# Ring slots 64 bytes longer, transposed rows 64 bytes apart: a four-layer transformer trunk on one Trainium2 core

## The chip, the cores and the metric

The kernel runs on one core of one Trainium2 chip, as one launch. The metric is the device time of one execution in microseconds (us). Engines are named as in the profile: PE is TensorE (matrix products), PEld its weight loads, DVE is VectorE, ACT is ScalarE, POOL is GpSimd, SP issues most of the DMAs.

## The reference, cut to what matters

A decoder trunk of four layers over 256 positions and a model width of 1024, all in float32. Layer i uses one token mixer (i mod 3: differential attention, stick-breaking attention, windowed attention with sinks), and then a SwiGLU feed-forward block of hidden width 2816. Each sub-layer sits between two RMS norms:

```python
for i in range(DEPTH):                                   # 4
    hn = rms_norm(x, norm_gains[i, 0])
    m = mixer[i % 3](hn, ...)                            # h @ w_in, attention, @ w_out
    x = x + rms_norm(m, norm_gains[i, 1])
    f = swiglu(rms_norm(x, norm_gains[i, 2]), w_gate[i], w_up[i], w_down[i])
    x = x + rms_norm(f, norm_gains[i, 3])

def swiglu(h, w_gate, w_up, w_down):
    return (jax.nn.silu(h @ w_gate) * (h @ w_up)) @ w_down
```

Nearly all of the arithmetic is in the products with the weights, and these are read once from memory: some 200 MB in float32.

## The kernel before, in words

The 256 positions are two **streams** of 128 rows, s = 0 and s = 1. Both run through all layers; stream 1 follows stream 0 by at most LAG = 8 weight units, so that each weight is loaded and prepared once and used by both.

**Weights.** The weights are cut into 378 units of 128 partitions by 1024 float32 (4096 bytes a partition). `load_dma` brings unit u into one of four `stage` tiles. `split` makes two tiles out of it in a ring of RING = 11 slots each: ACT copies the unit into `hi`, of type float32r, which rounds it, and DVE subtracts, so that `lo = stage - hi` holds what the rounding took away.

**Activations.** `pre_norm` transposes a stream's rows on PE and splits them in the same way into `xh` (high part) and `xl` (low part), 128 partitions by 8 blocks of 128. The feed-forward block's hidden rows become `hTh` and `hTl`, the attention outputs `oh` and `ol`.

**Products.** A product with weights is three float32r matmuls: high rows by `hi`, high rows by `lo`, low rows by `hi`. The weights are the moving operand (512 columns as a rule, 256 in the projections of layer 2), the transposed rows are the stationary one, a block of 128 by 128 loaded by a weight load of its own ahead of each matmul. `project` does the projections and gate/up, six matmuls a unit and stream: for each of two blocks `xh` by `hi` and `xh` by `lo`, then twice `xl` by `hi`. `rows_product` does the output projection and the down projection, six matmuls a unit and stream too. From the code there are 72 units of the first kind in layers 0, 1 and 3, 44 x 4 gate/up units, 8 x 4 output units and 22 x 4 down units, each used by both streams: 864 + 2112 + 384 + 1056 = 4416 matmuls of 512 columns; layer 2 adds 10 units of 24 matmuls over both streams with 256 columns, 240.

**Where the tiles lie.** Pools lay their tiles out one after another along each partition. Ring slots, stage tiles, `xh` and `xl` take 4096 bytes, the temporaries of the tag `t2k` 2048 (TMP = 8 buffers, which rotate in the order of allocation), `junk` 2048, the `o` tiles 2048. So before the change all operands of these matmuls start a multiple of 512 bytes apart. `junk` takes the elementwise output of sums of squares, which nobody reads; it has one buffer, and ACT alone writes it.

**Order.** `Emitter` emits both streams in the order of a simple model of PE's time: a stream that needs a weight unit goes on when the unit is in the ring, and tasks (transposes, scores, values of the attention) are spawned with a delay. `act`, `dve`, `pool` and `pe` are wrapped in `Start`: while its switch is on (until stream 1's first norm) instructions keep program order, after that the framework's scheduler may move them; its model decides the order within each engine's queue. On the chip each queue runs strictly in that order.

In the profile nearly every instruction has one line, that of the wrapper (L181), so groups are told apart by tiles: `mm_f` is gate/up, `acc_f` the down projection, `mm_a`, `mm_b`, `mm_c` projections of the mixers, `acc_a` and so on their output projections, `tp` transposes of x, `th_f` transposes of the hidden rows.

Of the kernel before, what the change touches and what calls it, by code (L numbers as in the profile page):

```python
# [10 lines left out]
F32R = mybir.dt.float32r  # L11
BF16 = mybir.dt.bfloat16
# [6 lines left out]
P = 128  # L19
D = 1024  # L20
KT = D // P
# [6 lines left out]
THETA = 10000.0  # L28

RING = 11  # L30
STAGE = 4
AHEAD = 3
LAG = 8
TMP = 8
# [6 lines left out]
class Emitter:  # L41
# [27 lines left out]
    def advance(self):  # L69
        free = self.pos[1] + RING  # L70
        while self.loaded < min((self.pos[0] + AHEAD if self.pos[0] else 2), free, self.limit):
            self.fetch(self.loaded + STAGE)
            self.ring[self.loaded] = self.split(self.loaded)
            self.loaded += 1
# [83 lines left out]
def trunk_kernel(ctx, tc, x, positions, norm_gains, a_w_in, a_w_out, a_lambda, a_subln, b_w_in, b_w_out,  # L158
                 c_w_in, c_w_out, c_sinks, w_gate, w_up, w_down, out, depth=DEPTH):
    nc = tc.nc  # L160
    cst = ctx.enter_context(tc.tile_pool(name="cst", bufs=1))
    ringp = ctx.enter_context(tc.tile_pool(name="ringp", bufs=RING))
    stagep = ctx.enter_context(tc.tile_pool(name="stagep", bufs=STAGE))
    wk = ctx.enter_context(tc.tile_pool(name="wk", bufs=2))
    sm = ctx.enter_context(tc.tile_pool(name="sm", bufs=2))
# [2 lines left out]
    def bank(tag, s, shape, name):  # L168
        return ps.tile(shape, F32, tag=f"{tag}{s}", name=name, bufs=BANKS[tag])
# [82 lines left out]

    def split(u):
        t = staged.pop(u)
        hi = ringp.tile([P, 1024], F32R, tag="hi", name=f"hi_{u}")
        lo = ringp.tile([P, 1024], F32R, tag="lo", name=f"lo_{u}")
        act.activation(hi, t, AF.Copy)
        dve.tensor_tensor(lo, t, hi.bitcast(F32), ALU.subtract)
        return hi, lo

    em = Emitter(load_dma, split, len(units), edges)


# [109 lines left out]
    def mm(o, a, b, start, stop, f32=False):  # L373
        pe.matmul(o, a, b, start=start, stop=stop)
        n = 1
        for d in o.shape[1:]:
            n *= d
        em.t += n * COLUMN_NS * (4 if f32 else 1)
# [6 lines left out]
    def transpose(o, i):  # L385
        pe.transpose(o, i, ident)
        em.t += P * COLUMN_NS * 4

    def rstd_of(name, s, ss, more=EPS, extra=None):

        u = sm.tile([P, 1], F32, tag=f"u{s}", name=f"u_{name}")
        r = sm.tile([P, 1], F32, tag=f"r{s}", name=f"r_{name}", bufs=3)
        pool.tensor_scalar(u, ss, more, extra, ALU.add, *([ALU.add] if extra else []))
        pool.tensor_tensor(r, u, mhalf[:, 0:1], ALU.pow)
        return r

    def first_halves(s, tps, gs, th, tl, name):

        ys = []
        for half in range(2):  # L400
            y = wk.tile([P, 4, P], F32, tag="t2k", name=f"y_{name}_{half}", bufs=TMP)
            dve.tensor_tensor(y, tps[half], gs[half].unsqueeze(2).to_broadcast([P, 4, P]), ALU.mult)
            ys.append(y)
            if s == 0:
                next(rope_tables)
        for half in range(2):
            hs = slice(4 * half, 4 * half + 4)
            act.activation(th[:, hs, :], ys[half], AF.Copy)
            dve.tensor_tensor(tl[:, hs, :], ys[half], th[:, hs, :].bitcast(F32), ALU.subtract)
            if s == 0:  # L410
                for _ in rope_tables if half else range(2):
                    next(rope_tables, None)
                em.limit = half + 1
                em.advance()
        em.limit = len(units)

    def pre_norm(s, n, name):

        ss = sm.tile([P, 1], F32, tag=f"ss{s}", name=f"ss_{name}")
        th = wk.tile([P, KT, P], F32R, tag=f"xh{s}", name=f"xh_{name}", bufs=1)  # L420
        tl = wk.tile([P, KT, P], F32R, tag=f"xl{s}", name=f"xl_{name}", bufs=1)
        tps, gs = [], []
        for half in range(2):
            tp = bank(("tp", "mm")[half], s, [P, 4, P], f"tp_{name}_{half}")
            for j in range(4):
                kt = 4 * half + j
                transpose(tp[:, j, :], xs[s][:, kt * P:(kt + 1) * P])
            tps.append(tp)
            gs.append(gains[:, n * KT + 4 * half:n * KT + 4 * half + 4])
        if act.on:  # L430
            first_halves(s, tps, gs, th, tl, name)
        else:
            for half in range(2):
                for j in range(4):
                    act.activation(th[:, 4 * half + j, :], tps[half][:, j, :], AF.Copy, scale=gs[half][:, j:j + 1])
                for j in range(4):
                    kt = 4 * half + j
                    dve.scalar_tensor_tensor(tl[:, kt, :], tps[half][:, j, :], gs[half][:, j:j + 1], th[:, kt, :].bitcast(F32),
                                             ALU.mult, ALU.subtract)
        junk = wk.tile([P, D], BF16, tag="junk", name=f"junk_{name}", bufs=1)  # L440
        act.activation(junk, xs[s], AF.Square, scale=1.0 / 32, accum_out=ss)
        return th, tl, rstd_of(name, s, ss)

# [11 lines left out]

    def post_norm(s, acc, gain, name):
        ss = sm.tile([P, 2], F32, tag=f"ssp{s}", name=f"ssp_{name}")
        junk = wk.tile([P, D], BF16, tag="junk", name=f"junk_{name}", bufs=1)
        mg = [wk.tile([P, 512], F32, tag="t2k", name=f"mg_{name}{h}", bufs=TMP) for h in range(2)]
        for h in range(2):  # L460
            act.activation(junk[:, h * 512:(h + 1) * 512], acc[h], AF.Square, scale=1.0 / 32, accum_out=ss[:, h:h + 1])
        r = rstd_of(name, s, ss[:, 0:1], ss[:, 1:2], EPS)
        for h in range(2):
            dve.tensor_tensor(mg[h], acc[h], gain[:, h * 512:(h + 1) * 512], ALU.mult)
        for h in range(2):
            cs = slice(h * 512, (h + 1) * 512)
            dve.scalar_tensor_tensor(xs[s][:, cs], mg[h], r, xs[s][:, cs], ALU.mult, ALU.add)
# [95 lines left out]
    def split_rows(oT, sl, src, scale=None):  # L563

        hi, lo = oT[0][:, sl, :], oT[1][:, sl, :]
        if scale is None:
            act.activation(hi, src, AF.Copy)
            dve.tensor_tensor(lo, src, hi.bitcast(F32), ALU.subtract)
        else:
            act.activation(hi, src, AF.Copy, scale=scale)  # L570
            dve.scalar_tensor_tensor(lo, src, scale, hi.bitcast(F32), ALU.mult, ALU.subtract)

    def layer_a(s, i, xn):
        inst = i // 3
        name = f"a{i}{s}"
# [64 lines left out]
        def values(g):  # L640
            yield ("e", (name, "w", g))
            if s:
                yield ("e", (f"a{i}0", "v", g))
            yield ("d", 500)
            o = bank("tp", s, [P, 4, P], f"pv_{name}{g}")
            for h in range(4):
                for kb in range(nk):
                    mm(o[:, h, :], wT[g][:, h, kb, :], V[g, kb][:, h * P:(h + 1) * P], kb == 0, kb == nk - 1, True)
            ss = sm.tile([P, 4], F32, tag=f"os{s}", name=f"os_{name}{g}")
            junk = wk.tile([P, D], BF16, tag="junk", name=f"junk_{name}{g}", bufs=1)  # L650
            for h in range(4):
                act.activation(junk[:, h * P:(h + 1) * P], o[:, h, :], AF.Square, accum_out=ss[:, h:h + 1])
            dve.scalar_tensor_tensor(ss, ss, 1.0 / P, st[g, "el"], ALU.mult, ALU.add)
            pool.tensor_tensor(ss, ss, mhalf[:, 0:4], ALU.pow)
            on = wk.tile([P, 4, P], F32, tag="t2k", name=f"on_{name}{g}", bufs=TMP)
            dve.tensor_tensor(on, o, ss.unsqueeze(2).to_broadcast([P, 4, P]), ALU.mult)
            yield ("d", 4200)
            tp = bank("tp", s, [P, 4, P], f"to_{name}{g}")
            for h in range(4):
                transpose(tp[:, h, :], on[:, h, :])  # L660
            split_rows(oT[g], slice(0, 4), tp, gsub[:, inst:inst + 1])
            yield ("d", 900)
            for h in range(4):
                em.set((name, "o", 4 * g + h))
# [288 lines left out]
```

## Time and profile before

| | us |
|---|---|
| median of 2 runs (1204.61 to 1205.26) | 1204.93 |
| the profiled execution | 1205.73 |
| its span, first to last instruction | 1203.9 |
| PE busy | 1185.8 (98%) |
| PE weight loads busy | 971.6 (81%) |
| DVE busy | 779.2 (65%) |
| ACT busy | 656.9 (55%) |

The granted clock of TensorE was 0.998 over the span. A busy share of PE counts from a matmul's start to its modelled end, so matmuls overlap in it; how fast PE goes is read from one start to the next. Idle time of DVE and ACT costs nothing as long as PE does not wait for them. The profiled execution's time is 1.8 us above its span.

### The profile page before, as it was taken

What the parts mean: (1) busy time and instruction counts of PE and PEld (TensorE: products, weight loads), DVE (VectorE), ACT (ScalarE), POOL (GpSimd) and SP (SyncE); (2) the same over time, 40 slices, a digit from 0 to 9 for tenths busy, and PEclk for the clock granted to TensorE, in tenths of its full rate; (3) what the DMA queues carried; (4) which work ended last, traced back from release to release, by engine and by line L of the source; (5) the groups of instructions that cost most, each with busy time, mean ns of one, the idle gap of its engine ahead of it and who ended that gap; (6) DMA issues with size and microseconds to landing.
All of it is one profiled execution on the core that took longest, in us unless ns stands there. A gap on an engine that the chain in (4) does not pass through costs nothing.

```text
span 1203.9 us, 16738 instructions
## 1 busy us (share of the span) xinstructions
PE 1185.8 (98%) x6028; PEld 971.6 (81%) x6028; DVE 779.2 (65%) x1217; ACT 656.9 (55%) x1197; POOL 48.1 (4%) x141
## 2 busy tenths in 40 slices
PE   8999999999999999999999999999999999999997
PEld 7787888888878888888888778888888788888886
DVE  7876765555847666555588666655587776655553
ACT  5665644444756665444476655444475565544442
POOL 2000100000200000000000000000010001000000
PEclk9999999999999999999999999999999999999999
DMA  8635465565644546656664246555565453566550
GB/s 280 206 120 159 151 192 186 189 192 179 225 139 123 176 140 193 191 181 189 192 199 135 88 144 191 191 189 187 185 205 156 129 175 123 179 189 192 180 170 35
DMA packets 140838, 205.90 MB, mean 171 GB/s; under 512 B 9554, under 2 KB 104916, under 8 KB 140756
## 3 DMA queue, kind: packets, MB, share of 16 engines
q1 hardware_dynamic: 140048, 204.51, 54.0%
q8 instruction: 47, 0.77, 0.3%
q10 hardware_dynamic: 708, 0.34, 0.1%
q14 instruction: 35, 0.29, 0.1%
HBM read 203.76 MB, written 1.05 MB: 170 GB/s over the span
## 4 chain that ended last, share of the span: by engine, by line
PE 90%; DVE 3%; ACT 3%; issue 2%; POOL 1%; DMA 1%; ACTq 0%; DVEq 0%; POOLq 0%
PE mm_f L181 39%; PE acc_f L181 18%; PE acc_a L181 3%; PE mm_c L181 2%; PE acc_b L181 2%; PE sc_a L181 2%; PE th_f L181 2%; DVE lo L181 1%; PE acc_c L181 1%; PE sc_b L181 1%; DMA stage<-in_a_w_in_dram 1%; ACT hi L181 1%; PE pv_a L181 1%; PE sc_c L181 1%; PE pv_c L181 1%
## 5 line engine op out<-in xcount | busy, mean ns | idle before, releaser
L181 DVE TENSOR_TENSOR lo<-stage,hi 128x1024 fp32r<-128x1024 f32 x378 | 461.0, 1223 | 285.5 <-ACT hi L181 283.6
L181 ACT ACTIVATE hi<-stage 128x1024 fp32r<-128x1024 f32 x378 | 399.5, 1061 | 324.1 <-PE mm_f L181 154.4
L181 PE MATMUL mm_f<-hi,xh_q 128*128 128x512 f32 x704 | 280.2, 398 | 0.0
L181 PE MATMUL mm_f<-lo,xh_q 128*128 128x512 f32 x704 | 274.5, 390 | 0.0
L181 PE MATMUL mm_f<-hi,xl_q 128*128 128x512 f32 x704 | 217.4, 390 | 1.0 <-DVE xl_q L181 1.0
L181 PEld LDWEIGHTS mm_f<-hi,xl_q 128*128 128x128 f32 x704 | 132.2, 188 | 30.4 <-DVE xl_q L181 1.9
L181 PEld LDWEIGHTS mm_f<-hi,xh_q 128*128 128x128 f32 x704 | 132.2, 188 | 26.1 <-ACT xh_q L181 0.2
L181 PEld LDWEIGHTS mm_f<-lo,xh_q 128*128 128x128 f32 x704 | 132.4, 188 | 25.8
L181 PE MATMUL acc_f<-hi,hTh_f 128*128 128x512 f32 x352 | 113.7, 399 | 0.5 <-ACT hTh_f L181 0.5
L181 PE MATMUL acc_f<-hi,hTl_f 128*128 128x512 f32 x352 | 111.4, 392 | 0.5 <-DVE hTl_f L181 0.4
L181 PE MATMUL acc_f<-lo,hTh_f 128*128 128x512 f32 x352 | 110.7, 390 | 0.0
L181 ACT ACTIVATE t_f<-mm_f,half_f 128x256 f32<-128x256 f32 x88 | 41.7, 474 | 79.7 <-PE mm_f L181 79.7
L181 PEld LDWEIGHTS acc_f<-hi,hTl_f 128*128 128x128 f32 x352 | 65.9, 188 | 14.9 <-DVE hTl_f L181 1.0
L181 PEld LDWEIGHTS acc_f<-lo,hTh_f 128*128 128x128 f32 x352 | 66.1, 188 | 14.0
L181 PEld LDWEIGHTS acc_f<-hi,hTh_f 128*128 128x128 f32 x352 | 63.7, 188 | 11.9 <-ACT hTh_f L181 0.8
L181 DVE SCALAR_TENSOR_TENSOR t_f<-t_f,mm_f 128x256 f32<-128x256 f32 x88 | 36.7, 417 | 35.2 <-ACT t_f L181 35.1
L181 DVE SCALAR_TENSOR_TENSOR h_f<-t_f,hsq_f,mm_f 128x256 f32<-128x256 f32 x88 | 42.3, 480 | 2.7
L181 ACT ACTIVATE hTh_f<-th_f 128x256 fp32r<-128x256 f32 x88 | 33.0, 375 | 17.0 <-PE th_f L181 16.7
L181 DVE TENSOR_TENSOR hTl_f<-th_f,hTh_f 128x256 fp32r<-128x256 f32 x88 | 36.5, 418 | 5.6 <-ACT hTh_f L181 5.3
L181 ACT ACTIVATE e_a<-sc_a,nm_a 128x128 f32<-128x128 f32 (+1 forms) x64 | 26.0, 420 | 17.1 <-DVE nm_a L181 16.9
L181 PE MATMUL th_f<-ident,h_f 128*128 128x128 f32 x176 | 33.5, 271 | 0.0
L181 PEld LDWEIGHTS th_f<-ident,h_f 128*128 128x128 f32 x176 | 24.1, 139 | 11.4 <-DVE h_f L181 0.3
(584 smaller groups left out, 1543.1 us busy)
## 6 DMA issues: line engine op xcount, KB each, us to landing
stage<-in_ffn_w_gate_dram SPq DMA_DIRECT2D x176, 256.0 KB, 2.9
stage<-in_ffn_w_up_dram SPq DMA_DIRECT2D x176, 256.0 KB, 3.1
stage<-in_ffn_w_down_dram SPq DMA_DIRECT2D x88, 512.0 KB, 3.5
stage<-in_a_w_in_dram SPq DMA_DIRECT2D x48, 512.0 KB, 3.8
stage<-in_b_w_in_dram SPq DMA_DIRECT2D x24, 512.0 KB, 3.6
stage<-in_a_w_out_dram SPq DMA_DIRECT2D x16, 512.0 KB, 3.9
stage<-in_c_w_in_dram SPq DMA_DIRECT2D x10, 512.0 KB, 3.6
gain<-in_norm_gains_dram SPq DMA_DIRECT2D x8, 512.0 KB, 4.1
```

Source lines behind the costliest of these rows:

```text
L181: i = call(*args, **kw)
```

## The change: what it does

Three edits.

- **The ring.** Each of the 22 tiles of the ring gets a tag of its own, with one buffer, instead of 11 rotating buffers of the tags `hi` and `lo`. A tile has 1040 elements, of which 1024 are used, so each takes 4160 bytes, and `hi` and `lo` of a slot now lie beside each other. The last slot's `hi` has 80 elements more (320 bytes). The ring is as deep as before. Counted in steps of 64 bytes modulo 512, ring tiles now start at all eight places.
- **The rows.** `xl` of stream 0 takes 4160 bytes, so that all that lies behind it, with stream 1's `xh` and `xl`, is shifted by 64 bytes more. Counted in the same steps, stream 0's `xh` and `xl` start at place 5 and stream 1's at place 6; before, all started at place 2, as did every ring tile.
- **The space.** `junk` loses its own 2048 bytes and takes a buffer of the rotating tag `t2k` at each use.

```diff
+SLOT = 1040
...
-    ringp = ctx.enter_context(tc.tile_pool(name="ringp", bufs=RING))
+    ringp = ctx.enter_context(tc.tile_pool(name="ringp", bufs=1))
...
     def split(u):
         t = staged.pop(u)
-        hi = ringp.tile([P, 1024], F32R, tag="hi", name=f"hi_{u}")
-        lo = ringp.tile([P, 1024], F32R, tag="lo", name=f"lo_{u}")
+        hi, lo = (ringp.tile([P, SLOT + pad], F32R, tag=f"{n}{u % RING}", name=f"{n}_{u}")[:, :1024]
+                  for n, pad in (("hi", 80 * (u % RING == RING - 1)), ("lo", 0)))
         act.activation(hi, t, AF.Copy)
         dve.tensor_tensor(lo, t, hi.bitcast(F32), ALU.subtract)
         return hi, lo
...
         th = wk.tile([P, KT, P], F32R, tag=f"xh{s}", name=f"xh_{name}", bufs=1)
-        tl = wk.tile([P, KT, P], F32R, tag=f"xl{s}", name=f"xl_{name}", bufs=1)
+        tl = wk.tile([P, SLOT if s == 0 else D], F32R, tag=f"xl{s}", name=f"xl_{name}", bufs=1)
+        tl = tl[:, :D].rearrange("p (k n) -> p k n", n=P)
...
-        junk = wk.tile([P, D], BF16, tag="junk", name=f"junk_{name}", bufs=1)
+        junk = wk.tile([P, D], BF16, tag="t2k", name=f"junk_{name}", bufs=TMP)
```

The last pair of lines stands at three places: `pre_norm`, `post_norm` and the values of layers 0 and 3.

The number and kinds of instructions on every engine stay the same. The scheduler's order changes at a few places, most of them in the first 60 us; POOL and SP keep theirs. The first is in ACT's queue, where the first four weight units have been copied and stream 1's first norm begins. The names are those of the text above with the unit's number (`hi_5` is unit 5; `xh_n01` is stream 1's first `xh`, in two halves; the last number only counts tiles). Before:

```order
L181 ACTIVATE hi_2_286<-stage_2_236 128x1024
L181 ACTIVATE hi_3_292<-stage_3_238 128x1024
L181 ACTIVATE xh_n01_297<-y_n01_0_309 128x512
L181 ACTIVATE xh_n01_297<-y_n01_1_311 128x512
L181 ACTIVATE junk_n01_317,ss_n01_296<-x_1_111 128x1024
L181 ACTIVATE hi_4_331<-stage_4_251 128x1024
L181 ACTIVATE hi_5_368<-stage_5_284 128x1024
L181 ACTIVATE hi_6_380<-stage_6_290 128x1024
```

And now, in the same place of ACT's queue:

```order
L182 ACTIVATE hi_2_286<-stage_2_236 128x1024
L182 ACTIVATE hi_3_292<-stage_3_238 128x1024
L182 ACTIVATE hi_5_368<-stage_5_284 128x1024
L182 ACTIVATE xh_n01_297<-y_n01_0_309 128x512
L182 ACTIVATE xh_n01_297<-y_n01_1_311 128x512
L182 ACTIVATE junk_n01_317,ss_n01_296<-x_1_111 128x1024
L182 ACTIVATE hi_4_331<-stage_4_251 128x1024
L182 ACTIVATE hi_6_380<-stage_6_290 128x1024
```

The copy of unit 5 now stands ahead of stream 1's rows, and ahead of unit 4. DVE's queue follows at the same place of the program; before:

```order
L181 TENSOR_TENSOR y_n01_0_309<-tp_n01_0_299,gains_191 128x512
L181 TENSOR_TENSOR y_n01_1_311<-tp_n01_1_304,gains_191 128x512
L181 TENSOR_TENSOR xl_n01_298<-y_n01_0_309,xh_n01_297 128x512
L181 TENSOR_TENSOR xl_n01_298<-y_n01_1_311,xh_n01_297 128x512
L181 TENSOR_TENSOR t1_a000q_384<-mm_a000q_277,crq_a00_269 128x512
```

And now, where `t1_a000q` (the first rotated queries of stream 0) comes later:

```order
L182 TENSOR_TENSOR y_n01_0_309<-tp_n01_0_299,gains_191 128x512
L182 TENSOR_TENSOR y_n01_1_311<-tp_n01_1_304,gains_191 128x512
L182 TENSOR_TENSOR lo_5_369<-stage_5_284,hi_5_368 128x1024
L182 TENSOR_TENSOR xl_n01_298<-y_n01_0_309,xh_n01_297 128x512
L182 TENSOR_TENSOR xl_n01_298<-y_n01_1_311,xh_n01_297 128x512
```

Here `lo` of unit 5 has moved ahead of both halves of stream 1's `xl`.

More of the change, by code (lines that the diff above doesn't have):

```diff
@@ L457, in post_norm @@
         ss = sm.tile([P, 2], F32, tag=f"ssp{s}", name=f"ssp_{name}")
-        junk = wk.tile([P, D], BF16, tag="junk", name=f"junk_{name}", bufs=1)
+        junk = wk.tile([P, D], BF16, tag="t2k", name=f"junk_{name}", bufs=TMP)
         mg = [wk.tile([P, 512], F32, tag="t2k", name=f"mg_{name}{h}", bufs=TMP) for h in range(2)]
@@ L649, in values @@
             ss = sm.tile([P, 4], F32, tag=f"os{s}", name=f"os_{name}{g}")
-            junk = wk.tile([P, D], BF16, tag="junk", name=f"junk_{name}{g}", bufs=1)
+            junk = wk.tile([P, D], BF16, tag="t2k", name=f"junk_{name}{g}", bufs=TMP)
             for h in range(4):
```

## The prediction

> **What bounds the kernel now.** I read the page first: busy times, the clock by slices, the chain that ended last.
>
> ```profile
> span 1203.9 us, 16738 instructions
> PE 1185.8 (98%) x6028; PEld 971.6 (81%) x6028; DVE 779.2 (65%) x1217; ACT 656.9 (55%) x1197; POOL 48.1 (4%) x141
> PEclk9999999999999999999999999999999999999999
> PE 90%; DVE 3%; ACT 3%; issue 2%; POOL 1%; DMA 1%; ACTq 0%; DVEq 0%; POOLq 0%
> L181 DVE TENSOR_TENSOR lo<-stage,hi 128x1024 fp32r<-128x1024 f32 x378 | 461.0, 1223 | 285.5 <-ACT hi L181 283.6
> L181 ACT ACTIVATE hi<-stage 128x1024 fp32r<-128x1024 f32 x378 | 399.5, 1061 | 324.1 <-PE mm_f L181 154.4
> L181 PE MATMUL mm_f<-hi,xh_q 128*128 128x512 f32 x704 | 280.2, 398 | 0.0
> L181 PE MATMUL mm_f<-hi,xl_q 128*128 128x512 f32 x704 | 217.4, 390 | 1.0 <-DVE xl_q L181 1.0
> ```
>
> PE is busy 98% of the span and 90% of the chain. DVE and ACT are idle 35% and 45% of the time; DVE's `lo` waits for ACT's `hi`, and half of the wait of `hi` is for PE, which frees ring slots: the ring is full, and weights are not what PE waits for. In the two groups of gate/up matmuls shown the idle time of PE is 0.0 and 1.0 us over 704 instructions each. So the time is PE's pace, and a change pays only through that pace, or through PE's few stalls.
>
> The pace is read from starts, in the timeline of PE, in the middle of a feed-forward block and just behind it (columns: start, length, what, count):
>
> ```profile
> 300.56 0.39 PE L181 MATMUL mm_f<-hi,xh_q 128*128 128x512 f32 x1
> 301.02 0.39 PE L181 MATMUL mm_f<-hi,xh_q 128*128 128x512 f32 x1
> 301.47 0.62 PE L181 MATMUL mm_f<-hi,xl_q 128*128 128x512 f32 x2
> 302.83 0.62 PE L181 MATMUL acc_f<-hi,hTl_f 128*128 128x512 f32 x2
> 303.88 0.48 PE L181 MATMUL mm_f<-hi,xh_q 128*128 128x512 f32 x1
> 304.20 0.39 PE L181 MATMUL mm_f<-lo,xh_q 128*128 128x512 f32 x1
> 305.36 0.61 PE L181 MATMUL acc_f<-hi,hTh_f 128*128 128x512 f32 x2
> ```
>
> From 300.56 to 302.83 ten matmuls of 512 columns start (four by `xh`, two by `xl`, four by `hTh`): 2.27 us, 227 ns each (226.9 in a longer stretch below). The 4416 such matmuls make 4416 x 0.2269 = 1002 us, 83% of the span. After small transposes have come between, from 304.20 to 305.36, five starts take 1.16 us, 232 ns each, before the old pace is back. Layer 2 has matmuls of 256 columns, and the first microseconds ran slower:
>
> ```profile
> 670.64 0.28 PE L181 MATMUL mm_c<-hi,xh_n 128*128 128x256 f32 x1
> 671.36 0.64 PE L181 MATMUL mm_c<-hi,xl_n 128*128 128x256 f32 x4
> 11.43 0.63 PE L181 MATMUL mm_a000q<-hi,xh_n 128*128 128x512 f32 x1
> 12.29 1.05 PE L181 MATMUL mm_a000q<-hi,xl_n 128*128 128x512 f32 x2
> 1189.69 0.62 PE L181 MATMUL acc_f<-hi,hTh_f 128*128 128x512 f32 x2
> 1193.32 0.62 PE L181 MATMUL acc_f<-hi,hTl_f 128*128 128x512 f32 x2
> ```
>
> At 670 us six starts take 0.72 us, 120 ns each for 256 columns; near the end sixteen starts take 3.63 us, 226.9 ns each. So 256 more columns cost 226.9 - 120 = 106.9 ns, and each matmul carries 120 - 106.9 = 13.1 ns that its columns don't explain. At 11.43 us two starts take 0.86 us, 430 ns each, where the columns alone, 213.8 ns at the later pace, would take 428 at half of it: at that slow pace hardly anything of the 13.1 ns shows. Those 13.1 ns are the stake of this change. While a matmul streams its weights out of SBUF, the load of the next stationary block reads there too; if these two reads get in each other's way, addresses can matter. Stake: (4416 + 240) x 13.1 ns = 61 us.
>
> **The change, part by part.** *Places of operands.* Before, every float32r operand starts a multiple of 512 bytes from every other one. Within that, the ten matmuls quoted mix all that there is: `hi` and `lo`, first and second half of a slot (2048 bytes apart), two streams, rows of three tiles, and the pace doesn't move. Whole multiples of 512 bytes do nothing, then. Steps of 64 bytes below 512 don't occur before, so the trace can't show their price directly, and I bound it by rows from both sides. Below: all 13.1 ns gone, -61 us. Above: each matmul at the disturbed pace of 232 ns, 4416 x (232 - 226.9) ns = +23 us. I take 0, for two reasons. A matmul of 512 columns reads 2048 bytes while the weight load beside it reads 512, so the moving read runs through every place modulo 512 four times, wherever either starts: a shift of the start changes when they meet, not how often. And the undisturbed pace comes back by itself after an upset, and the same one in both stretches quoted: a state that the two reads settle into by timing would take in a fixed shift as well.
>
> The Trainium skill, "SBUF — State Buffer", section Specifications, gives lines of 16 bytes as the unit in which engines read, with a penalty for each access that crosses to a new line; steps of 64 bytes keep every operand at the start of such a line, so by that rule the sum gets 0 from this edit. The same page of the Trainium skill, section Who interferes with whom, has it that "PE and ACT never wait on anyone", which leaves the 13.1 ns of the rows above without a cause; the trace neither bears the rule out nor breaks it.
>
> *ACT and DVE on the new places.* `hi` takes 1061 ns and `lo` 1223 ns; both engines have a third of the span and more to spare. 5% on either would be 20 or 23 us of work beside PE: nothing on the path.
>
> *`junk` in the rotating buffers.* Nothing is added but waits: a square now waits for whoever last used a buffer handed out eight allocations ago. Each square is itself behind the product or the update that it squares, later than those old readers; 0, and at most some tenths of a microsecond at a norm, where PE goes on with the other stream. Per-tile tags of the ring keep its depth; ACT gains waits for its own long-finished copies: 0.
>
> *The order at the start.* Here there is a price. ACT's queue has `hi_5` ahead of stream 1's `xh`, and DVE's queue `lo_5` ahead of its `xl`. When does unit 5 land? The queue of SP, the window of that issue, and the engines around it:
>
> ```profile
> 13.12 0.38 SPq L246 DMA_DIRECT2D stage<-in_a_w_in_dram  x1
> stage<-in_a_w_in_dram SPq DMA_DIRECT2D x1, 512.0 KB, 6.2
> 14.11 1.06 ACT L181 ACTIVATE hi<-stage 128x1024 fp32r<-128x1024 f32 x1 [0.27 <-DMA stage<-in_a_w_in_dram]
> 17.54 1.23 ACT L181 ACTIVATE xh_n<-y_n 128x512 fp32r<-128x512 f32 x2 [2.37 <-DVE y_n L181]
> 18.20 1.30 DVE L181 TENSOR_TENSOR xl_n<-y_n,xh_n 128x512 fp32r<-128x512 f32 x2
> 19.39 0.39 PE L181 MATMUL mm_a010q<-hi,xh_n 128*128 128x512 f32 x1
> 21.61 1.22 DVE L181 TENSOR_TENSOR lo<-stage,hi 128x1024 fp32r<-128x1024 f32 x1
> ```
>
> The sixth issue, at 13.12, landed 6.2 us later, at 19.3. ACT then waits from 15.2 to 19.3, copies unit 5 until 20.4, and has the first half of `xh` (half of 1.23 us) at about 21.0; PE wants it at 19.39: 1.6 us of stall. `lo_5` then holds DVE from 20.4 to 21.6, the first half of `xl` is there at about 22.3, wanted four matmuls after 21.0, at 21.9: 0.4 us more. What is queued behind on ACT, `hi_4`, moves behind the square, to some 23 us, and `lo_4` from 21.61 to some 24; PE needs them a dozen matmuls (2.7 us) after 21.4, so they hardly bind, and the stage buffer that `lo_4` frees delays unit 8, which is wanted ten microseconds later. Loss: 2.0 us. What could take it back are PE's own stalls a little later:
>
> ```profile
> 38.19 0.72 PE L181 MATMUL sc_a<-kT_a,qT_a 64*128 64x128 f32 x8 [0.78 <-ACT kT_a L181]
> PE mm_a001k L181 <- DVE t_a001q L181: 0.7, 1, 0.7
> ```
>
> They sum to 1.5 us and hang on data that would be as late as PE itself in part; I give back 0.5. So the start costs 1.5 us, with bounds of -0.5 (both stalls closed by the new order and no loss) and 3 (the transfers bind too).
>
> **Sum.** Span 1203.9 + 0 + 1.5 = 1205.4. The profiled execution took 1205.73, 1.8 above its span and 0.8 above the median of 1204.93. On the median: 1204.9 + 1.5 = 1206.4 us.
>
> **The rivals.** *Faster: the 13.1 ns are a collision of equal places.* Then they go where places differ. For it: each matmul has them, with 512 and with 256 columns alike, they don't grow with the columns, and they are not there at the slow pace, as a collision of two reads would be hidden when one has time to spare; and before, all operands share one place out of eight. Against it: the argument of the four rounds, and that half of the stationary loads beside a matmul could be at the start and the other anywhere, yet the pace is one number. Gone altogether: 1206 - 61 = 1145. Gone for half of the pairs: 1206 - 30 = 1176. Only a fifth gone: 1194. "TensorE: Matmul & The Clock Gate" of the Trainium skill, section Wait — 56ns, gives 215.7 ns from start to start at 512 columns. The rows here show 226.9, against it; if different places brought PE to that page's pace, the change would be worth 4416 x 11.2 ns = 49 us, an estimate from that page: 1157.
>
> *Slower: the settled state is lost.* The rows at 304.20 show that there is a worse pace than 226.9, and that it takes undisturbed matmuls to get back. Now each switch from `hi` to `lo` (64 bytes), between slots and between streams shifts the places of the two reads against each other. If that keeps upsetting them, PE stays at 232 ns: 4416 x 5.1 ns = 23 us, 1229. It decides from 5.2 ns a matmul on (23 us and the start's 1.5 make 2%). Partly upset, 1 to 4 ns: 1211 to 1224. Against it: before, the operands change too at every matmul, and nothing is upset by that.
>
> *The change does nothing to PE and the start comes out even*: 1204.5, within the forecast's own range of 1204 to 1209.
>
> **How the numbers follow.** Pace unchanged, with the loss at the start: 0.60, 1204 to 1209, likeliest 1206. Faster by collisions gone: 0.24, spread from 1145 to 1204, two thirds of it beyond 2% (under 1181, about what a measurement of this kernel surely tells from no change), since a collision that depends on the place should go for more than half of the pairs. Slower by the lost state: 0.16, from 1210 to about 1236 (the 232 ns are a mean over five starts, and may be 1 or 2 ns short of the worst), some 0.07 beyond 2% (1229). So faster 0.16, same 0.77, slower 0.07. The range from 1178 to 1232 leaves out some 0.15 below and 0.05 above.
>
> **What would show it.** In the timeline of PE around 300 us: starts 226.9 ns apart, with `hi` and `lo`, both streams and all slots alike, show the first step right; 214 to 224 or a mixture that goes by slot shows the faster rival, 230 and more in stretches without transposes the slower. `hi` at 1061 ns and `lo` at 1223 ns should stand. At the start PE should wait for ACT's `xh_n` near 20 us by one to two microseconds, and ACT's `hi` ahead of it for its DMA. The prediction is wrong if the time leaves 1204 to 1209 with an unchanged pace: then the waits of `junk`, or the order, cost what I put at nothing.

## The result, and the profile after

| | before | after |
|---|---|---|
| median of 2 runs each, us | 1204.93 | 1224.05 (1223.28 to 1224.81) |
| the profiled execution, us | 1205.73 | 1224.81 |
| its span, us | 1203.9 | 1223.0 |

The changed kernel takes 1.0159 times as long, 95% interval 1.0138 to 1.0179: 19.1 us slower. The time lies in the range forecast (1178 to 1232), but outside the likeliest case's own range of 1204 to 1209.

The page of the changed kernel, the rows that answer to those of before:

```profile
span 1223.0 us, 16751 instructions
PE 1201.7 (98%) x6028; PEld 971.7 (79%) x6028; DVE 779.1 (64%) x1217; ACT 657.5 (54%) x1197; POOL 45.1 (4%) x141
PEclk8999999999999999999999999999999999999999
PE 88%; DVE 5%; ACT 2%; DMA 2%; issue 1%; POOL 1%; DVEq 0%; POOLq 0%; ACTq 0%
L182 DVE TENSOR_TENSOR lo<-stage,hi 128x1024 fp32r<-128x1024 f32 x378 | 461.0, 1223 | 299.0 <-ACT hi L182 297.9
L182 ACT ACTIVATE hi<-stage 128x1024 fp32r<-128x1024 f32 x378 | 399.5, 1061 | 339.0 <-PE mm_f L182 159.7
L182 PE MATMUL mm_f<-hi,xh_q 128*128 128x512 f32 x704 | 282.6, 401 | 0.0
```

DVE's `lo` and ACT's `hi` take what they took, 1223 and 1061 ns, and the weight loads are as long in sum (971.7 us). Busy PE alone has grown, from 1185.8 to 1201.7 us, with the same number of matmuls, and the group of `mm_f` by `hi` and `xh_q` still has no idle time. So the time went into the matmuls themselves. The timeline of PE around 300 us (columns: start, length, what, count):

```profile
301.11 0.39 PE L182 MATMUL mm_f<-hi,xh_q 128*128 128x512 f32 x1
301.34 0.40 PE L182 MATMUL mm_f<-lo,xh_q 128*128 128x512 f32 x1
301.57 0.40 PE L182 MATMUL mm_f<-hi,xh_q 128*128 128x512 f32 x1
301.81 0.39 PE L182 MATMUL mm_f<-lo,xh_q 128*128 128x512 f32 x1
302.04 0.63 PE L182 MATMUL mm_f<-hi,xl_q 128*128 128x512 f32 x2
302.51 0.63 PE L182 MATMUL acc_f<-hi,hTh_f 128*128 128x512 f32 x2
302.97 0.62 PE L182 MATMUL acc_f<-lo,hTh_f 128*128 128x512 f32 x2
303.44 0.63 PE L182 MATMUL acc_f<-hi,hTl_f 128*128 128x512 f32 x2
303.90 0.39 PE L182 MATMUL mm_f<-hi,xh_q 128*128 128x512 f32 x1
```

Twelve matmuls start between 301.11 and 303.90: 2.79 us, 232.5 ns each, where before it was 226.9. No small transposes stand between them; it is the undisturbed pace that is worse. Over the whole trace, from the starts of neighbouring 512-column matmuls (those less than 300 ns apart, some 4000 pairs), the mean is 231.73 ns against 228.03 before: 3.70 ns more, and 4416 x 3.70 ns = 16.3 us. Before, most stretches repeat steps of 227, 227 and 226 ns; after, nearly all steps lie between 224 and 241 ns, and they settle nowhere. The mean covers the pairs without a transpose between them, so 16.3 us is an estimate: the 4005 pairs alone make 14.8. This kind of mean over the starts is what "mean pace" says below.

The rest is at the start. ACT and PE of the changed kernel, from their timelines, and the busy times by windows (columns: window, its length, busy time and count of PE, PEld, DVE, ACT, POOL, then the granted clock, DMA share, GB/s):

```profile
19.67 1.06 ACT L182 ACTIVATE hi<-stage 128x1024 fp32r<-128x1024 f32 x1 [4.20 <-DMA stage<-in_a_w_in_dram]
20.63 1.14 ACT L182 ACTIVATE xh_n<-y_n 128x512 fp32r<-128x512 f32 x2
21.30 0.51 PE L182 MATMUL mm_a010q<-hi,xh_n 128*128 128x512 f32 x1 [2.00 <-ACT xh_n L182]
21.30:22.60 1.30, 1.30 (x4) 0.67 (x4) 1.30 (x3) 1.30 (x2) 0.00 (x0) 0.82 0.04 14
22.60:25.90 3.30, 3.30 (x9) 2.62 (x9) 2.53 (x7) 3.30 (x6) 1.65 (x3) 0.55 0.50 166
128.88 0.40 PE L182 MATMUL mm_f<-hi,xh_q 128*128 128x512 f32 x1
```

The same window and the same matmul (the first of layer 0's feed-forward block) before:

```profile
22.60:25.90 3.30, 3.30 (x16) 2.75 (x15) 3.30 (x9) 2.49 (x4) 1.63 (x1) 1.00 0.54 158
125.38 0.39 PE L181 MATMUL mm_f<-hi,xh_q 128*128 128x512 f32 x1
```

ACT waits 4.20 us for unit 5, PE waits 2.00 us for the rows behind it, and then, from 22.6 to 25.9, PE has 9 matmuls at work where it had 16 (one or two of them begun before 22.6), at a granted clock of 0.55 against 1.00. By 125 us the changed kernel is 3.5 us behind; the other 15.6 us of the span's 19.1 come behind that.

### The profile page after: what moved, and what is told of

It is laid out like the page before. It is cut to its first block, busy times and chain, and to the rows that moved or that the text cites. A ratio compares the mean times of both kernels' runs of the same rounds, so it can differ in the third digit from the quotient of the medians.

```text
span 1223.0 us, 16751 instructions
## 1 busy us (share of the span) xinstructions
PE 1201.7 (98%) x6028; PEld 971.7 (79%) x6028; DVE 779.1 (64%) x1217; ACT 657.5 (54%) x1197; POOL 45.1 (4%) x141
## 4 chain that ended last, share of the span: by engine, by line
PE 88%; DVE 5%; ACT 2%; DMA 2%; issue 1%; POOL 1%; DVEq 0%; POOLq 0%; ACTq 0%
PE mm_f L182 39%; PE acc_f L182 18%; PE acc_a L182 3%; DVE lo L182 2%; PE acc_b L182 2%; PE sc_a L182 2%; PE th_f L182 2%; PE acc_c L182 1%; PE mm_c L182 1%; DMA stage<-in_a_w_in_dram 1%; PE sc_b L182 1%; ACT hi L182 1%; PE pv_a L182 1%; PE sc_c L182 1%; DVE x L182 1%
## 5 line engine op out<-in xcount | busy, mean ns | idle before, releaser
L182 DVE TENSOR_TENSOR lo<-stage,hi 128x1024 fp32r<-128x1024 f32 x378 | 461.0, 1223 | 299.0 <-ACT hi L182 297.9
L182 ACT ACTIVATE hi<-stage 128x1024 fp32r<-128x1024 f32 x378 | 399.5, 1061 | 339.0 <-PE mm_f L182 159.7
L182 PE MATMUL mm_f<-hi,xl_q 128*128 128x512 f32 x704 | 220.8, 395 | 0.8 <-DVE xl_q L182 0.8
L182 PEld LDWEIGHTS acc_f<-lo,hTh_f 128*128 128x128 f32 x352 | 66.1, 188 | 15.6
L182 ACT ACTIVATE hTh_f<-th_f 128x256 fp32r<-128x256 f32 x88 | 33.1, 376 | 18.4 <-PE th_f L182 18.1
L182 ACT ACTIVATE e_a<-sc_a,nm_a 128x128 f32<-128x128 f32 (+1 forms) x64 | 26.1, 421 | 18.4 <-DVE nm_a L182 18.1
```

Of the source, the lines that this page charges most:

```text
L182: i = call(*args, **kw)
```

## The experiments

Two theories stood at first. **S**, "a lost state": PE settles into 226.7 ns only where the place of the rows against the weights never changes; any fixed shift would do, and the change keeps shifting. **D**, "distance": each distance between the start of the stationary operand (rows) and that of the moving one (weights) has a pace of its own, and 0 is a good one. A third, **W**, blames the waits and the order, not the places.

### 1. The change without its 64 bytes

```diff
-SLOT = 1040
+SLOT = 1024
...
-                  for n, pad in (("hi", 80 * (u % RING == RING - 1)), ("lo", 0)))
+                  for n, pad in (("hi", 0), ("lo", 0)))
```

> The changed kernel with slots of 4096 bytes, no longer last slot and no longer xl: per-slot tags, junk in the rotating buffers and the new order stay, but all operands start a multiple of 512 bytes apart again. If the places alone make the 19 us: about 1206 (226.9 ns a matmul again, with the 1.5 us of the start). If junk's waits, the tags or the order cost it: about 1224.

Measured: 1208.89 us, ratio 1.0029 (1.0017 to 1.0040) against 1205.31 beside it. Mean pace 227.88 ns. So the tags, the order and `junk` together cost 3.6 us, and the 64 bytes the rest: 1.0159 against 1.0029 is 1.3% of 1205, 15.7 us. W explains a fifth of the loss.

### 2. and 3. The ring's 64 bytes alone, the rows' alone

```diff
-        tl = wk.tile([P, SLOT if s == 0 else D], F32R, tag=f"xl{s}", name=f"xl_{name}", bufs=1)
+        tl = wk.tile([P, D], F32R, tag=f"xl{s}", name=f"xl_{name}", bufs=1)
```

> The changed kernel without the 64 bytes between the two streams' rows: only the ring is spread, hi and lo of a slot and the slots among themselves 64 bytes apart modulo 512. Theory of the settled state (each change of the relative place from one matmul to the next upsets the pace, and hi and lo alternate at nearly every matmul): the pace stays near 231.7 ns, 1221 to 1225. Theory of prices by place (each distance between stationary and moving operand has its own price): odd and even distances are as frequent as before, so about the same 1220 to 1225.

For the rows alone: slots of 1024 elements as in the first experiment, and stream 0's `xl` with 1040.

> The changed kernel with the ring flat and only stream 1's rows (and both streams' o tiles of stream 0) 64 bytes on: the relative place changes only where PE goes from one stream or from one kind of rows to the other, every six to twelve matmuls. Settled state: an upset of some ten matmuls at each switch, so most of the loss stays, 1213 to 1222. Prices by place: two distances only, 0 and 64 bytes; 1206 if both are cheap, and any pace then changes by stream in a fixed way.

Measured: the ring alone 1222.64 us, ratio 1.0145 (1.0129 to 1.0160), mean pace 231.37 ns; the rows alone 1226.43, ratio 1.0175 (1.0160 to 1.0190), mean pace 232.44. Both keep the tags and `junk`, and so the 3.6 us of the first experiment. Either half alone brings the loss, and the two don't add up. With the rows alone there are two distances: 0 for `xh` and `xl` of stream 0, 64 bytes for stream 1 and for the hidden rows. Split by distance the mean pace is 230.7 ns at 0 and 233.3 ns at 64. The timeline of the rows alone shows the worst pace in a long undisturbed stretch:

```profile
299.64 0.39 PE L182 MATMUL mm_f<-hi,xh_q 128*128 128x512 f32 x1
...
302.44 0.39 PE L182 MATMUL mm_f<-hi,xh_q 128*128 128x512 f32 x1
...
305.24 0.39 PE L182 MATMUL mm_f<-hi,xh_q 128*128 128x512 f32 x1
```

Twelve matmuls each time, in 2.80 us: 233.3 ns, with no drift back to 226.7.

### 4. One constant distance of 64 bytes

The kernel before, and one gap ahead of all rows. No place changes within the run.

```diff
+        if name == "n00":
+            wk.tile([P, 16], F32, name="gap", bufs=1)
```

> The kernel before with a gap of 64 bytes ahead of all transposed rows: every stationary operand of the weight products stands 64 bytes further on modulo 512 than the moving one, the same for all, nothing alternates. Settled state: 226.9 ns as before, 1204 to 1206. Prices by place: one new pace for all, so anything from 1145 (no collision left) to 1225.

Measured: 1225.92 us, ratio 1.0171 (1.0156 to 1.0187). The timeline of PE:

```profile
299.03 0.40 PE L181 MATMUL mm_f<-hi,xh_q 128*128 128x512 f32 x1
...
301.83 0.40 PE L181 MATMUL mm_f<-hi,xh_q 128*128 128x512 f32 x1
...
304.63 0.40 PE L181 MATMUL mm_f<-hi,xh_q 128*128 128x512 f32 x1
```

2.80 us for twelve matmuls again, 233.3 ns. And PE does settle here: in steps of 231 and 236 ns by turns, through the whole block (mean pace 233.4). S has fallen: nothing ever shifts in this kernel, and it loses more than the change does. A settled state is not the same as a good one.

### 5. The same 64 bytes ahead of everything

```diff
+    cst.tile([P, 16], F32, name="gap")
```

> The kernel before with a gap of 64 bytes ahead of the ring: ring and rows all 64 bytes further on, so their distances stay multiples of 512 bytes, at another place. If the distance between the stationary and the moving operand counts: 226.9 ns a matmul and 1205. If the place of the rows itself counts (before a multiple of 128 bytes, now not): 233 ns and 1226 as with the rows alone moved.

Measured: 1204.58 us, ratio 0.9998 (0.9987 to 1.0009). The timeline:

```profile
300.40 0.62 PE L182 MATMUL acc_f<-hi,hTl_f 128*128 128x512 f32 x2
...
303.12 0.62 PE L182 MATMUL acc_f<-hi,hTl_f 128*128 128x512 f32 x2
```

2.72 us for twelve: 226.7 ns. Rings and rows have moved together, and nothing happens. What counts is the distance between the two operands, not where either lies. Nor is it their distance from the other tiles that are written meanwhile: in experiment 2 the rows and the `stage` tiles start at the same place modulo 512, in experiment 4 the ring and the `stage` tiles do, and both lose; rows against ring is what differs in both.

### 6., 7. and 8. The pace by distance

In three kernels the rows of each layer's mixer and feed-forward block get a distance of their own, so one run shows several. The ring has 10 slots here, to make room. The table's numbers are elements of 4 bytes; the diff shows `xh` alone, and `xl`, the `o` tiles and the hidden rows are placed in the same way. Sixth:

```diff
-RING = 11
+RING = 10
...
+PLACE = {'m0': 80, 'f0': 32, 'm1': 112, 'f1': 64, 'm2': 16, 'f2': 96, 'm3': 0, 'f3': 48}
...
+        th = wk.tile([P, 1152], F32R, tag=f"xh{s}", name=f"xh_{name}", bufs=1)
+        th = th[:, placed(name)[0]].rearrange("p (k n) -> p k n", n=P)
...
```

> The kernel before with the rows' tiles 512 bytes longer and the rows at an offset in them that goes by layer: mixers of layers 0, 1, 2, 3 at 320, 448, 64, 0 bytes, feed-forward blocks at 128, 256, 384, 192 bytes; ring of 10 slots for the space. One pace is read for each section. If the distance counts, each section settles at a pace of its own: 227 at 0, 233 at 64, and the others anywhere from 214 to 240; a distance with less than 227 would make a faster kernel. If only a multiple of 128 bytes counts: 227 at 0, 128, 256, 384 and 233 at 64, 192, 320, 448. Total between 1205 and 1230.

Seventh, with another table:

```diff
+PLACE = {'m0': 112, 'f0': 4, 'm1': 24, 'f1': 8, 'm2': 32, 'f2': 12, 'm3': 1, 'f3': 80}
```

> The same with finer offsets: mixers of layers 0, 1, 2, 3 at 448, 96, 128 and 4 bytes, feed-forward blocks at 16, 32, 48, 320 bytes. If the pace goes by steps of 64 bytes: 227 at 4, 16, 32, 48 bytes, as at 0. If it goes smoothly with the distance: a part of the way from 227 to 233 at 16, 32, 48. 4 bytes is off a line of 16 bytes, so one more line a block is read: by that alone some ns more.

Eighth:

```diff
+PLACE = {'m0': 62, 'f0': 60, 'm1': 58, 'f1': 56, 'm2': 48, 'f2': 52, 'm3': 63, 'f3': 40}
```

> The kernel before, with a ring of 10 slots, in which the rows of each layer and kind of block lie at another distance ahead of the place of the weights: feed-forward blocks of layers 0 to 3 at 240, 224, 208 and 160 bytes, mixers of layers 0, 1, 3 at 248, 232, 252, the mixer of layer 2 at 192. So far, from start to start of 512-column matmuls: 226.7 ns at 0 and 256 bytes, 232 to 234 at 4 to 128, and 229 at 192 and 448. Theory A, the pace rises slowly on the side just below a multiple of 256: 208 to 252 bytes lie between 226.7 and 229 ns, 160 between 229 and 233, and the time is 1206 to 1213. Theory B, only equal places are good and 192 is an exception: 208 to 252 bytes show 231 to 234 ns, and the time is 1220 to 1227. Theory C, some distance is better than equal places: under 226 ns in one of the blocks.

Measured: 1216.31, 1226.22 and 1223.52 us, one execution each and so without an interval (1205.0, 1205.0 and 1205.08 for the kernel before beside them). Rows of the sixth kernel's timeline in the blocks with 128, 256 and 192 bytes, a pair for each, twelve matmuls apart:

```profile
200.36 0.63 PE L187 MATMUL acc_f<-hi,hTl_f 128*128 128x512 f32 x2
...
203.16 0.63 PE L187 MATMUL acc_f<-hi,hTl_f 128*128 128x512 f32 x2
...
539.91 0.61 PE L187 MATMUL mm_f<-hi,xl_q 128*128 128x512 f32 x2
...
542.63 0.61 PE L187 MATMUL mm_f<-hi,xl_q 128*128 128x512 f32 x2
...
1099.96 0.39 PE L187 MATMUL mm_f<-hi,xh_q 128*128 128x512 f32 x1
...
1102.71 0.39 PE L187 MATMUL mm_f<-hi,xh_q 128*128 128x512 f32 x1
```

2.80, 2.72 and 2.75 us: 233.3 ns at 128 bytes, 226.7 at 256, 229.2 at 192, within one run. The mean paces of the feed-forward blocks, some 740 pairs of starts each, transposes between the matmuls included:

| distance, bytes | mean pace, ns |
|---|---|
| 0 (before, four blocks) | 227.5 to 228.0 |
| 256 | 227.6 |
| 240 | 228.4 |
| 192 | 229.0 |
| 16, 32, 48 | 232.7, 233.2, 233.3 |
| 64, 320 | 233.4, 233.4 |
| 128, 384 | 233.0, 232.5 |
| 160, 208, 224 | 233.2, 233.0, 233.4 |

The mixers have more transposes between, and their projections (some 240 pairs each) stand at 228.7 to 229.1 for 0. Against that: 229.7 and 229.9 at 448 bytes, 231.4 at 232, 232.3 at 4, 233.5 to 233.9 at 96, 248, 252 and 320. The pattern repeats after 256 bytes: 0 as 256, 64 as 320, 128 as 384, 192 as 448. Equal places are the best of all that were tried. Just below a multiple of 256 the pace is not a slope that leads up to it: 240 and 192 are nearly good, 208, 224, 248 and 252 are bad, 232 lies between. Of the eighth run's theories B comes nearest, with its time too (1220 to 1227), though 240 is a second exception; the slope of A is not there, and no distance has the steady pace under 226 ns of C.

### 9. `junk` in the rotating buffers, alone

The kernel before with the `junk` lines of the change, nothing else.

> The kernel before with the third edit alone: the squares' unread output takes a rotating buffer at each use. The copy of unit 5 and its lo stay where they were at the start; PE's order is that of before. If the third edit's waits cost nothing, and the 3.9 us that the changed kernel without its 64 bytes took more than before are all the start's order: 1204 to 1206. If the waits of the squares cost a part of them: 1206.5 to 1209.

Measured: 1205.14 us against 1205.08, ratio 1.0002 (0.9992 to 1.0011). `junk` costs nothing.

### 10. Two distances by turns

The kernel before with 64 bytes between the block of `hi` slots and that of `lo` slots; the rows lie at the place of `lo`.

```diff
+        if u == 0:
+            ringp.tile([P, 16], F32, name="gap", bufs=1)
```

> The kernel before with 64 bytes between the block of hi slots and the block of lo slots; all rows lie at the place of lo. Each product thus goes between two distances: the two thirds of matmuls whose moving operand is hi have 64 bytes, the third with lo has 0. Theory A, each matmul takes the pace of its own distance: about 233.4 ns for hi and 227 to 228 ns for lo, mean 231.4, and 1204.9 + 4416 x 3.4 ns = 1220. Theory B, the pace carries over from the matmuls ahead, so that a change of the distance upsets it: hi and lo alike, at 231 to 234 ns, with no run of 226 and 227 ns in the feed-forward blocks; 1218 to 1230.

Measured: 1216.25 us, one execution (1205.34 for before beside it). The timeline:

```profile
299.87 0.40 PE L181 MATMUL mm_f<-hi,xh_q 128*128 128x512 f32 x1
...
302.65 0.39 PE L181 MATMUL mm_f<-hi,xh_q 128*128 128x512 f32 x1
```

Twelve in 2.78 us, 231.7 ns. Over the trace the mean pace is 230.9 ns for matmuls with `hi` (at 64 bytes) and 230.4 for those with `lo` (at 0), each counted to the next start; where the distance stays what it is, the same two groups have 233.7 at 64 (experiment 4) and 228.3 at 0 (before). So a matmul does not have the pace of its own distance, and its neighbours' distances matter too: theory A's split did not show. But the time is below what either theory expected. Two thirds at 233.7 and one third at 228.3 would be 231.9; the mean over both groups is 230.7. The switch by itself adds no loss here.

### 11. The ring's tags alone

```diff
-    ringp = ctx.enter_context(tc.tile_pool(name="ringp", bufs=RING))
+    ringp = ctx.enter_context(tc.tile_pool(name="ringp", bufs=1))
...
-        hi = ringp.tile([P, 1024], F32R, tag="hi", name=f"hi_{u}")
+        hi = ringp.tile([P, 1024], F32R, tag=f"hi{u % RING}", name=f"hi_{u}")
-        lo = ringp.tile([P, 1024], F32R, tag="lo", name=f"lo_{u}")
+        lo = ringp.tile([P, 1024], F32R, tag=f"lo{u % RING}", name=f"lo_{u}")
```

> The kernel before with nothing but a tag of its own for each ring tile (slots of 4096 bytes, all places as before, the squares' output as before). Unit 5's copy moves ahead of stream 1's first rows, as in the changed kernel. If this order is what costs the 3.9 us that the changed kernel without its 64 bytes took more than before: 1207.5 to 1209.5, with PE waiting for the rows by 1.4 to 2 us near 20 us and a pace above 400 ns for some three microseconds behind it. If the order costs only the stall: 1206 to 1207.

Measured: 1209.35 us, ratio 1.0034 (1.0023 to 1.0046), mean pace 228.07 ns. PE's timeline, the window behind the stall, and the first gate/up matmul:

```profile
21.33 0.79 PE L181 MATMUL mm_a010q<-hi,xh_n 128*128 128x512 f32 x1 [2.89 <-ACT xh_n L181]
21.30:26.60 5.30, 5.27 (x12) 4.13 (x13) 4.53 (x9) 5.30 (x7) 1.65 (x3) 0.50 0.35 110
129.40 0.39 PE L181 MATMUL mm_f<-hi,xh_q 128*128 128x512 f32 x1
```

The order that the tags bring, with unit 5's copy ahead of stream 1's rows, is enough for the loss at the start: 129.40 against 125.38 is 4.0 us, and the span is 4.0 us longer (1207.9 against 1203.9). Nothing is added after 129 us.

### 12. The other sign for 256 columns

With 256 columns 64 bytes are better, not worse. Starts in layer 2's mixer of experiment 4:

```profile
650.15 0.28 PE L181 MATMUL mm_c<-hi,xh_n 128*128 128x256 f32 x1
...
650.83 0.28 PE L181 MATMUL mm_c<-hi,xh_n 128*128 128x256 f32 x1
```

Six matmuls in 0.68 us, 113 ns each, where before they took 120. So: the kernel before, with `junk` in the rotating buffers for room, and only that mixer's rows at 64 bytes (the diff shows `xh`; `xl` goes the same way).

```diff
+        at = 16 if name[:2] == "n2" else 0
+        th = wk.tile([P, D + 64], F32R, tag=f"xh{s}", name=f"xh_{name}", bufs=1)
+        th = th[:, at:at + D].rearrange("p (k n) -> p k n", n=P)
...
```

> The kernel before with the squares' unread output in the rotating buffers (which gives room) and the rows of layer 2's mixer 64 bytes past the place of the weights, all other rows at equal places modulo 256. The 240 matmuls of 256 columns took 126.0 ns from start to start on the mean at equal places and 122.0 where all rows lay 64 bytes off: 240 x 4.0 ns = 1.0 us less, 1204.0 against 1205.0, if each kind of matmul has its own best distance and nothing else changes. If the 512-column matmuls around suffer from the switch, 1205 or more.

Measured: 1204.55 us against 1205.43, ratio 0.9994 (0.9985 to 1.0003). The mean over these 256-column matmuls went from 126.0 to 121.9 ns, as expected. In the time the gain has its expected size, 0.9 us, but the interval includes no change: as a faster kernel it is not shown.

## Why the prediction was right or wrong

The time lies in the range, but that is owed to the slower rival, which had 0.16; the mechanism held likeliest, 0.60, an unchanged pace with the loss at the start, accounts for a fifth of what was lost.

**What bounds the kernel** was right: PE's pace, and the change paid, or cost, through that pace and PE's stalls.

**"Places of operands: I take 0" is the step that failed.** It was 15.7 us (the change against experiment 1), inside the bounds worked out there, -61 to +23. Both reasons for the 0 were wrong. "A shift of the start changes when they meet, not how often": experiment 4 shifts only the start, by one constant, and costs 20.6 us, so a fixed shift of the start does change the pace, whatever it does to how often the two reads meet. "A state that the two reads settle into by timing would take in a fixed shift as well": PE does settle under the fixed shift, but into 231 and 236 ns by turns. The rows quoted for the first step showed one distance, 0, repeated at multiples of 512 bytes; "whole multiples of 512 bytes do nothing" was read right (256 do nothing either), and it said nothing of the steps below.

By the rule of 16-byte lines (the Trainium skill, "SBUF — State Buffer", section Specifications) steps of 64 bytes cost nothing. The paces above don't follow lines: 16, 32 and 64 bytes, whole lines, have 232.7 to 233.4 ns, and 4 bytes, which cuts a line, is no worse at 232.3 (in a mixer).

**The slower rival** gave the size: it put a partly upset pace, 1 to 4 ns, at 1211 to 1224, and the measured 3.70 ns and 1224.05 us stand at its upper end. The likeliest case was the wrong one of the two. The rival's mechanism was half right. The argument against it, that operands change at every matmul before and nothing is upset, did not bear on it: what changes before keeps its distance. Switches that keep upsetting a good state are not needed for a loss: a distance that never switches is worse (experiment 4), and one that switches between 0 and 64 lies between the two (experiment 10). But they are at work in the changed kernel, which spreads the products over all eight distances in steps of 64 bytes: sorted by their own distance modulo 256 (from the tiles' places in the program, each matmul counted to the next start), its matmuls stand at 232.2 ns for 0, 231.2 for 64, 232.2 for 128 and 231.1 for 192, so those at 0 have lost 4.5 ns against their constant pace and those at 64 have gained 2.2. A plain mean of the constant paces in the table, in equal shares, is (227.7 + 233.4 + 232.8 + 229.0) / 4 = 230.7 ns; measured were 231.7. Why it is 1.0 ns above stays open.

**The faster rival**, a collision of equal places, is refuted for 512 columns: of the distances tried, equal places modulo 256 have the best pace. The stake itself, 13.1 ns in each matmul whatever its columns, was not a fixed cost of a matmul: the same subtraction at 64 bytes (233.3 ns for 512 columns, 113.3 for 256) leaves 113.3 - 120.0 = -6.7 ns. What sets the paces no run here shows. The 215.7 ns that the Trainium skill gives ("TensorE: Matmul & The Clock Gate", section Wait — 56ns) were reached at no distance: the best steady pace in any run is 226.7.

**ACT and DVE on the new places, and `junk`**: both put at 0, both right (1061 and 1223 ns; experiment 9).

**The order at the start** was the right mechanism with the wrong size: 1.5 us forecast, with 3 as the upper bound; 3.6 (experiment 1) to 4.0 us (experiment 11) measured, 3.5 in the trace of the changed kernel at its first gate/up matmul, some half a microsecond of it the worse pace. The stall came about as worked out: unit 5's copy was forecast to end at 20.4, and ACT goes on to `xh` at 20.63. That 2.0 us were forecast and 2.00 measured is partly luck: the forecast was 1.6 for `xh` and 0.4 for `xl`, the trace has one wait, for `xh`, and the same wait was 1.43 us in experiment 1 and 2.89 in experiment 11. What was missed comes behind it: PE's clock is granted at half (0.50 from 22.14 to 25.55), and the twelve matmuls of `mm_a010q` take 4.61 us (21.30 to 25.91) where they took 2.72 (19.39 to 22.11), 1.9 us more. The waits further on gave back little of that, where 0.5 had been put in.

The sum that should have stood there: 3.6 + 16.3, less (126.1 - 124.9) x 240 ns = 0.3 us for layer 2's 256 columns, is 19.6 us, or 18.1 with the 14.8 of the pairs alone; measured were 19.1.

## What to carry to other kernels

Where a kernel's time is the pace of matmuls with a weight load each, as here, the distance between the starts of the two operands is worth a trial: a pad of 64 bytes moved this kernel by 1.7% with no instruction changed. A constant distance is not enough; it has to be a good one. A trace in which all operands share one place says nothing of other places; the price of a step that never occurs in it has to be measured, and the argument that a shift "changes when they meet, not how often" is worth little where the loop has its own rhythm. Count a stall of PE with what comes after it, its slower clock, and look for order changes that come along with a change of tags.

## What the hardware showed that was not expected

- The pace of float32r matmuls with 512 columns depends on the distance between the starts of the stationary and the moving operand, with a period of 256 bytes as far as four pairs of distances show it: 226.7 ns at 0, in steps of 227, 227 and 226; 233.3 at 64, as 231 and 236 by turns in experiment 4 and as 233, 233 and 234 in experiment 3; at 192 a cycle of 226, 229 and 232. Moving both by 64 bytes changes nothing. Why these are the settled rhythms no run shows.
- The sign depends on the length: at 64 bytes a matmul of 512 columns is 6.6 ns slower than at 0 (233.3 against 226.7), one of 256 columns 7 ns faster (113 against 120).
- The pace of a matmul depends on the distances of its neighbours too: with two distances by turns both kinds run at 230.4 to 230.9 ns, and in the changed kernel all four distances modulo 256 at 231.1 to 232.2.
- A wait of PE can cost a second time, in its clock. In the changed kernel PE was idle for 2.00 us, started four more matmuls, and then the granted clock was 0.50 from 22.14 to 25.55 us. In experiment 1 a wait of 1.43 us was followed by 0.50 from 22.53 to 25.94. In experiment 11, with 2.89 us of idle time, the clock fell at 20.42, while PE still waited, and stayed at 0.50 until 27.25. The Trainium skill, "TensorE: Matmul & The Clock Gate", section What's actually happening, has the clock halve after at least one idle window of about 3.4 us; here 1.43 us of idle time were enough, which that figure would not have led one to expect.
